# The query projection of a hybrid encoder layer as two units of seven block products, with the scores of two heads between the second unit's products

## The chip, the cores and the metric

The kernel runs on one core of one Trainium2 chip (trn2). The metric is the device time of one execution in microseconds; lower is better. The profile comes from one profiled execution on the same core. TensorE is PE (its weight loads are PEld), VectorE DVE, ScalarE ACT, GpSimd POOL, SyncE SP; SP issues most DMAs, POOL those that add to their destination.

## The reference, cut to what matters

One layer: a mixer (an S5 scan and a gated MLP, merged by gates) whose output goes through w_out and is added to the residual x; cross-attention to 256 memory tokens; a SwiGLU FFN; a last norm. 512 tokens of 1024 channels, 4 attention heads of 256, all float32. What the change touches:

```
def memory_cross_attention(hn, memn, w_q, w_k, w_v, w_o):
    bsz, seq, _ = hn.shape
    q = (hn @ w_q).reshape(bsz, seq, XATTN_HEADS, XATTN_HEAD_DIM)
    k = (memn @ w_k).reshape(bsz, MEM_LEN, XATTN_HEADS, XATTN_HEAD_DIM)
    v = (memn @ w_v).reshape(bsz, MEM_LEN, XATTN_HEADS, XATTN_HEAD_DIM)
    s = jnp.einsum('blhd,bmhd->bhlm', q, k).astype(jnp.float32) * (XATTN_HEAD_DIM ** -0.5)
    p = jax.nn.softmax(s, axis=-1).astype(v.dtype)
    o = jnp.einsum('bhlm,bmhd->blhd', p, v).reshape(bsz, seq, D_MODEL)
    return o @ w_o
...
        h = h + merged @ w_out[i]
        h = h + memory_cross_attention(rms_norm(h, xattn_norm_g[i]), memn,
                                       w_q[i], w_k[i], w_v[i], w_xo[i])
        h = h + swiglu(rms_norm(h, ffn_norm_g[i]), w_gate[i], w_up[i], w_down[i])
```

## The kernel before, in words

Every large product runs as three matmuls on pairs of rounded halves. `split` (line 85) makes such a pair of a float32 tile: ACT casts it to `hi` (line 87), DVE subtracts to get `lo` (line 88); `mm3` (line 319) then multiplies hi by hi, hi by lo and lo by hi.

**Weights.** All weight blocks stand in one list, `plan`, in the order of their use. Each entry has its loads and how many entries ahead they are issued (`LOADS`, 3, for plain loads into `wraw`; 4 to 7 for the tiles `b` and `t` of the units), and a function that splits the block into `whi` and `wlo`, two entries ahead of its use (`SPLITS`, line 93). `raw`, `hi` and `lo` have three buffers each. `next_w` (line 294) hands out the next block and triggers the loads and splits that are due. `feat` (line 324) multiplies with the weights at rest and gives channels by tokens, `tokm` (line 361) with the tokens at rest and gives tokens by channels. `tick` (line 414) lets code that was put off by `later` (line 404) run after a given amount of PE work. Within that, the order on each engine is made by the tile framework's scheduler when the kernel is built.

**Stages around the change.** w_out with the residual and the norm into `hn` (transposed on PE into `ptr`, split by `to_feat`); w_k (`feat`, 8 blocks of 4 x 128 rows by 256 columns, 128x256 matmuls, as there are 256 memory tokens); w_v (`tokm`); then for each of four heads two blocks of w_q, the head's scores with the softmax, and the values of the head before (`values`, tiles `po`, result split into `ot`), the turn of the probabilities (`turn_probs`, transposes into `ppt`, split into `p`) put off by one tick. Then w_xo (`tokm`), with the last head's values as its hook, and the norm for the FFN.

**Units.** Gate and up run as ten units of Strassen's scheme in Winograd's form: a 1024 by 512 block of the weights in four quarters, the tokens in four quarters, seven products of 24 matmuls of 128x256 (`product`, line 1273) in place of eight, with sums of quarters made on DVE (the weights') or once (the tokens'). Down does the same over chunks; its weight sums are made in DRAM ahead of time: for each of 24 jobs SP copies a block inside DRAM into `dsum` and POOL's DMA adds a second one onto it. `plan_sums` (line 224) hangs these jobs on entries of `plan`: the copies on every third entry from `first_copy + 2`, each addition three entries later.

**Memory.** Tiles of long life lie in slots: `hn` and later `fn` in B, `mg_hi` and `ot_hi` in D, `mg_lo`/`ot_lo` in E. `APART` (48, 112) are two offsets by which the units' pairs of halves begin apart. PSUM has five banks for products and three for transposes.

Of the kernel before, what the change touches and what calls it, by code (L numbers as in the profile page):

```python
# [52 lines left out]
def hybrid_layer_kernel(  # L53
# [140 lines left out]

    def plan_units(units, down):
# [28 lines left out]
    def plan_sums(first, step):  # L224


        more = {5: lambda c: down_block(0, 1, c), 7: lambda c: down_block(1, 1, c),
                6: lambda c: down_sum(5, c), 4: lambda c: down_sum(6, c)}

        def start(q, i, jc, c):  # L230
            tc.keep_in_program_order(nc.sync.dma_start(down_sum(q, c), down_block(i, jc, c)))

        def add(q, c):
            nc.gpsimd.dma_start(down_sum(q, c), more[q](c), accum_op=ALU.add)

        j = first
        for q, i, jc in ((5, 0, 0), (7, 0, 1), (6, 1, 1), (4, 1, 0)):
            for c in range(CHUNKS):
                plan[j][1].append((0, lambda x=(q, i, jc, c): start(*x)))
                plan[j + step][1].append((0, lambda x=(q, c): add(*x)))  # L240
                j += step
# [39 lines left out]
    for c0 in range(0, D, 256):  # L281
        plan_feat(w_q, c0, KD)
# [8 lines left out]
    plan_sums(first_copy + 2, 3)  # L291
# [176 lines left out]
    def to_feat(src, hi, lo, tsl, full=None):  # L468

        for q in range(2):  # L470
# [4 lines left out]
            split(hi[:, 4 * q:4 * q + 4, tsl], lo[:, 4 * q:4 * q + 4, tsl], ps)  # L475
# [5 lines left out]
    def norm_feat(src, g, hi, lo, tsl, ss=None, full=None):  # L481
        xs = xsp[0].tile([P, D], F32, tag="xs", name="xs", bufs=2)
        rms_scale(src, g, xs, ss)
        later(0.6, lambda: to_feat(xs, hi, lo, tsl, full))
# [580 lines left out]
    hn_hi, hn_lo = token_slot("hn")  # L1065
    hn = (hn_hi, hn_lo)
# [16 lines left out]
    for t in range(NM):  # L1083
        later(0.2 + t, lambda t=t: mem_norm(t))

# [15 lines left out]
    def feat_norm(g, hi, lo, full=None):  # L1101
        return lambda t, ss: norm_feat(h[:, t, :], g, hi, lo, slice(t * P, (t + 1) * P), ss, full)

    mg = (mg_hi, mg_lo)
    for half in range(2):
        tokm(w_out, half * 512, mg, KD, add_evac(half, 0, feat_norm(g_x, hn_hi, hn_lo)))
# [3 lines left out]
    shift = ap_.tile([P, APART[0]], F32, name="shift")  # L1110
    nc.gpsimd.memset(shift, 0.0)
    kt_hi = ap_.tile([P, KD, M], F32R, name="kt_hi")
    kt_lo = ap_.tile([P, KD, M], F32R, name="kt_lo")
    vt_hi = ap_.tile([P, NM, D], F32R, name="vt_hi")
    vt_lo = ap_.tile([P, NM, D], F32R, name="vt_lo")
# [4 lines left out]
    def v_evac(half):  # L1120
        def f(t, ps):
# [417 lines left out]
```

## Time and profile before

| | |
|---|---|
| time, median of 3 runs | 915.74 us (913.55 to 921.12) |
| the profiled execution's own time | 915.13 us |
| its span in the profile | 913.4 us |
| PE busy / idle in the span | 899.4 / 14.0 us |
| DVE, ACT, POOL busy | 608.1, 458.8, 90.8 us |
| w_k | 418.33 to 443.26 us |
| w_v | 443.26 to 465.66 us |
| w_q, scores, values 0 to 2 | 465.66 to 532.80 us |
| w_xo and the FFN's norm | 532.80 to about 583.5 us |

The span is cut at the first and last instruction; what lies around it makes 1.7 us. Stages are cut where the chain of work that ended last goes from one tile name to the next. Busy times are of one engine; PE and PEld overlap. In a row of the chain stand the start, the length, the engine, what was written, the line and how many instructions; in a row of groups, after the bar, the busy time of all and the mean ns of one.

### The profile page before, as it was taken

To read this page: it belongs to the slowest core of one execution; us is meant where nothing else is said; L and a number is where in the kernel's file an instruction comes from. 1 tells how busy PE (TensorE), PEld (TensorE's weight loads), DVE (VectorE), ACT (ScalarE), POOL (GpSimd) and SP (SyncE) were. 2 spreads that over 40 slices of the span, in tenths; PEclk is the share of its full clock that TensorE was granted. 3 is DMA by queue.
4 is the path that set the end of the run, shared out by engine and by line. 5 is a ranking of instruction groups with operands and counts; after the bars stand their busy time and mean duration, and the time that the engine had idled before them with its cause. 6 is when DMAs were issued, how large, how long until landed. Compare 5 with 4: busy or idle time off the path is not lost.

```text
span 913.4 us, 14223 instructions
## 1 busy us (share of the span) xinstructions
PE 899.4 (98%) x5558; PEld 789.9 (86%) x5558; DVE 608.1 (67%) x1003; ACT 458.8 (50%) x671; POOL 90.8 (10%) x153
## 2 busy tenths in 40 slices
PE   9999999999999999999999999999999999999996
PEld 6788888888888887789898888899999999888885
DVE  6596662888753235858545544787778777889875
ACT  5542995244374334446434433655554554655663
POOL 1004210000025300002010001000000000000000
PEclk9999999999999999999999999999999999999998
DMA  7445273684546655776995217416456453246572
GB/s 252 128 127 142 81 176 114 189 202 128 149 136 155 147 180 161 238 240 192 262 275 137 81 59 238 108 43 160 123 148 146 122 158 98 70 144 200 198 240 83
DMA packets 105557, 142.25 MB, mean 156 GB/s; under 512 B 13185, under 2 KB 73105, under 8 KB 105490
## 3 DMA queue, kind: packets, MB, share of 16 engines
q1 hardware_dynamic: 90690, 120.67, 40.7%
q0 software_dynamic: 12064, 19.37, 12.9%
q10 hardware_dynamic: 2736, 1.31, 0.6%
q8 instruction: 43, 0.70, 0.3%
q14 instruction: 24, 0.20, 0.1%
HBM read 134.54 MB, written 29.85 MB: 180 GB/s over the span
## 4 chain that ended last, share of the span: by engine, by line
PE 86%; ACT 4%; DVE 3%; DMA 3%; issue 2%; POOL 1%; POOLq 0%; SPq 0%; ACTq 0%; DVEq 0%
PE pf L322 32%; PE pt L322 13%; PE px L1282 12%; PE pq L1282 6%; PE dx L322 5%; PE dq L322 3%; PE pv L1282 3%; PE dv L322 2%; PE pk L731 2%; DVE wlo L88 1%; PE ptr L474 1%; DMA b<-in_w_gate_dram 1%; PE po L322 1%; ACT whi L87 1%; PE psc L322 1%
## 5 line engine op out<-in xcount | busy, mean ns | idle before, releaser
L88 DVE TENSOR_TENSOR wlo<-wraw,whi 128x1024 fp32r<-128x1024 f32 x132 | 157.4, 1193 | 132.4 <-ACT whi L87 131.2
L87 ACT CAST whi<-wraw 128x1024 fp32r<-128x1024 f32 x132 | 135.7, 1029 | 178.1 <-PE pf L322 81.7
L322 PE MATMUL pf<-xn,whi 128*128 128x512 f32 x448 | 140.7, 393 | 0.0
L322 PEld LDWEIGHTS pf<-xn,whi 128*128 128x128 f32 x448 | 83.7, 188 | 17.3 <-issue 0.2
L322 PE MATMUL pf<-xn,wlo 128*128 128x512 f32 x224 | 87.5, 391 | 0.0
L1282 PE MATMUL px<-fn,whi 128*128 128x256 f32 x480 | 83.7, 277 | 0.0
L1282 PEld LDWEIGHTS px<-fn,whi 128*128 128x128 f32 x480 | 72.7, 188 | 0.3 <-ACT u L1394 0.2
L87 ACT CAST whi<-b 128x1024 fp32r<-128x1024 f32 x40 | 42.2, 1054 | 54.5 <-PE px L1282 26.6
L88 DVE TENSOR_TENSOR wlo<-b,whi 128x1024 fp32r<-128x1024 f32 x40 | 48.9, 1222 | 27.3 <-ACT whi L87 27.3
L1282 PE MATMUL px<-fn,wlo 128*128 128x256 f32 x240 | 66.3, 276 | 0.0
L322 PE MATMUL dx<-whi,s 128*128 128x512 f32 x170 | 53.9, 392 | 1.4 <-ACT whi L87 1.0
L1282 PE MATMUL pq<-s,whi 128*128 128x256 f32 x320 | 55.0, 276 | 0.0
L322 PEld LDWEIGHTS pf<-xn,wlo 128*128 128x128 f32 x224 | 42.1, 188 | 8.5
L1282 PEld LDWEIGHTS pq<-s,whi 128*128 128x128 f32 x320 | 48.4, 188 | 0.1
L88 DVE TENSOR_TENSOR wlo<-t,whi 128x1024 fp32r<-128x1024 f32 x30 | 36.7, 1224 | 16.8 <-ACT whi L87 16.8
L87 ACT CAST whi<-t 128x1024 fp32r<-128x1024 f32 x30 | 31.6, 1054 | 32.2 <-PE pv L1282 11.3
L1282 PEld LDWEIGHTS px<-fn,wlo 128*128 128x128 f32 x240 | 45.1, 188 | 0.0
L1282 PE MATMUL pq<-s,wlo 128*128 128x256 f32 x160 | 44.2, 276 | 0.0
L322 PE MATMUL pt<-whi,xn 128*128 128x512 f32 x128 | 42.2, 402 | 0.0
L322 PE MATMUL pf<-hn,whi 128*128 128x512 f32 (+1 forms) x160 | 41.8, 348 | 0.0
L322 PEld LDWEIGHTS dx<-whi,s 128*128 128x128 f32 x170 | 31.7, 188 | 8.5 <-ACT whi L87 1.2
L322 PE MATMUL dx<-wlo,s 128*128 128x512 f32 x85 | 33.2, 391 | 0.2 <-DVE wlo L88 0.2
(384 smaller groups left out, 2170.1 us busy)
## 6 DMA issues: line engine op xcount, KB each, us to landing
wraw<-in_w_in_dram SPq DMA_DIRECT2D x36, 512.0 KB, 4.1
dsum<-in_w_down_dram SPq DMA_DIRECT2D x20, 512.0 KB, 5.9
wraw<-dsum SPq DMA_DIRECT2D x20, 512.0 KB, 3.9
b<-in_w_gate_dram SPq DMA_DIRECT2D x15, 512.0 KB, 3.6
b<-in_w_up_dram SPq DMA_DIRECT2D x15, 512.0 KB, 3.8
wraw<-in_w_down_dram SPq DMA_DIRECT2D x15, 512.0 KB, 3.6
dsum<-in_w_down_dram POOLq DMA_DIRECT2D x10, 512.0 KB, 6.4
dsum<-dsum POOLq DMA_DIRECT2D x10, 512.0 KB, 7.2
```

The lines of the kernel that those rows point to most:

```text
L87: nc.scalar.copy(dst_hi, src)
L88: last_lo[0] = nc.vector.tensor_tensor(dst_lo, src, dst_hi.bitcast(F32), ALU.subtract)
L322: nc.tensor.matmul(ps, a[x], b[y], start=start and i == 0, stop=stop and i == 2, skip_group_check=free)
L474: nc.tensor.transpose(ps[:, j, :], src[:, k * P:(k + 1) * P], ident)
L731: nc.tensor.matmul(ps[32 * j:32 * j + 32, q, :], bd[i][:, g].rearrange("p d c -> p (d c)"), lc(es[i], g), start=(i == 0), stop=False, tile ...
L1282: nc.tensor.matmul(ps[:, j, :], a[x], b[y], start=start and j == k == i == 0, stop=k == 3 and i == 2, skip_group_check=True)
```

## The change

w_q goes the units' way. Its 1024 columns are two units (n = 0, 1) of 512, heads 0 and 1 and heads 2 and 3; each is seven products. In the plan the 8 blocks of w_q become 14.

- **Weight sums** of the four products that need one (`qsum`, q = 4 to 7) are made in DRAM, 8 jobs more. They go first in the jobs' list; the places are new: 16 jobs on every third entry from `first_copy - 4`, two at 71 and 75, and the last 14 of down's at every fifth entry from 104, which lies in gate and up.
- **Token sums.** ACT copies each transposed `ptr` of hn into `hfull`, unrounded; `token_sums` makes four sums of quarters (128x1024 each) on DVE and splits them (`hsd`, `hse`, in slots D and E, and hn's own place), put off into w_k and w_v. Two of hn's own splits fall away. `hn` now lies `APART`.
- **Order.** Products 1, 5, 2, 6 and so on of both units are interleaved, with copies (`seed`, `kept`) and subtractions (`minus`) between, each finished part split at once into the head's query (`query_part`). scores(0) stands between products 6 and 7 of the second unit, scores(1) after the last. As `ot` lies in D and E, which hold token sums until the last product, values(0) and (1), scores(2) and (3) and the turns follow it; values(2) and (3) are w_xo's hook.
- **Places.** `hfull` and the memory values (`vt`) share one buffer; the probabilities of the odd heads take a buffer of the tag `gain`, so g_f is loaded later.

The core of the diff (`product` and `unit_bank` moved up with it, with the operands as an argument):

```
+    QSRC = {1: (0, 0), 2: (1, 0), 3: (1, 1)}
+    qsum = {(q, n): dp.tile([P, KD // 2, 256], F32, name=f"qsum{q}{n}") for q in (4, 5, 6, 7) for n in range(2)}
...
+        for q, n in ((1, 0), (5, 0), (2, 0), (6, 0), (1, 1), (7, 0), (2, 1), (4, 0), (3, 0),
+                     (6, 1), (7, 1), (5, 1), (4, 1), (3, 1)):
...
+                nc.sync.dma_start(got["raw"], query_block(*QSRC[q], n) if q in QSRC else qsum[q, n])
...
-    plan_sums(first_copy + 2, 3)
+    plan_sums([(first_copy - 4 + 3 * i, 3) for i in range(16)] + [(71 + 4 * i, 3) for i in range(2)] +
+              [(104 + 5 * i, 4) for i in range(14)])
...
-            split(hi[:, 4 * q:4 * q + 4, tsl], lo[:, 4 * q:4 * q + 4, tsl], ps)
+            if q != skip:
+                split(hi[:, 4 * q:4 * q + 4, tsl], lo[:, 4 * q:4 * q + 4, tsl], ps)
             if full is not None:
                 nc.scalar.copy(full[:, 4 * q:4 * q + 4, tsl], ps)
...
-    hn_hi, hn_lo = token_slot("hn")
+    hn_hi, hn_lo = token_slot("hn", APART)
...
+    def token_sums():
+        h11, h12, h21, h22 = (hfull[:, k, t] for t in (T0, T1) for k in (K0, K1))
+        for q, dst, x, y, op in ((5, h22, h21, h22, ALU.subtract), (7, h21, h11, h21, ALU.subtract),
+                                 (6, h11, h22, h11, ALU.subtract), (3, h12, h12, h11, ALU.add)):
+            nc.vector.tensor_tensor(dst, x, y, op)
+            later(0.5 * len(sums), lambda q=q, dst=dst: split(*hops[q], dst))
+            sums.append(q)
...
+    later(2, token_sums)
...
+        prob = ap_.tile([P, NT, M], F32, tag="prob", name="prob", bufs=1) if hd % 2 == 0 else \
+            np_.tile([P, NT, M], F32, tag="gain", name="prob", bufs=2)
...
-    for hd in range(XH):
-        feat(w_q, hd * XD, hn, KD, q_evac, parts=2 if hd == 0 else 1)
-        probs = scores(hd)
-        if hd > 0:
-            values(hd - 1, *pts.pop(0))
-        later(1, lambda hd=hd, probs=probs: pts.append(turn_probs(hd, probs)))
...
+    query_product(x1, 1, 6)
+    u2 = kept(x1, "u2")
+    probs0 = scores(0)
+    query_part(2, T0, v1)
+    query_product(x1, 1, 7)
+    u3 = kept(x1, "u3")
+    qq_ = unit_bank("qq")
+    query_product(qq_, 1, 5, True)
+    u3 = minus(qq_, u3)
+    query_product(x1, 1, 4)
+    query_part(2, T1, x1)
+    turn(0, probs0)
+    query_product(qq_, 1, 3)
+    u2 = minus(qq_, u2)
+    probs1 = scores(1)
+    query_part(3, T1, u3)
+    query_part(3, T0, u2)
+    ot_hi = slot("D", (P, KD, T), F32R, "ot_hi")
+    ot_lo = slot("E", (P, KD, T), F32R, "ot_lo")
+    values(0, *pts.pop(0))
+    probs2 = scores(2)
+    turn(1, probs1)
+    probs3 = scores(3)
+    values(1, *pts.pop(1))
+    turn(2, probs2)
+    later(1, lambda: turn(3, probs3))
...
-    tokm(w_xo, 0, ot, KD, add_evac(0, 1, None), hook=lambda: values(XH - 1, *pts.pop()))
+    tokm(w_xo, 0, ot, KD, add_evac(0, 1, None), hook=lambda: [values(i, *pts.pop(i)) for i in (2, 3)])
```

The scheduler makes of it three new neighbourhoods that the prediction speaks of. The first is DVE in w_k. Before, a block's `wlo` alternates with the remainders of w_k's result (`kt_lo`) and of hn:

```order
L88 TENSOR_TENSOR wlo<-wraw,whi 128x1024 [waits DMAHW3_49,PE_49,Activation_49]
L88 TENSOR_TENSOR hn<-ptr,hn 128x4x128 [waits Activation_49]
L88 TENSOR_TENSOR kt_lo<-pf_3864,kt_hi 128x256 [waits Activation_49]
L452 TENSOR_SCALAR ms<-ms 128x1 [waits DVE_49]
L88 TENSOR_TENSOR hn<-ptr,hn 128x4x128 [waits Activation_49]
L88 TENSOR_TENSOR wlo<-wraw,whi 128x1024 [waits DMAHW5_49,PE_49,Activation_49]
```

Now, at the middle of w_k:

```order
L88 TENSOR_TENSOR hn<-ptr,hn 128x4x128 [waits Activation_49]
L1166 TENSOR_TENSOR hfull<-hfull 128x4x256 [waits Activation_49]
L88 TENSOR_TENSOR wlo<-wraw,whi 128x1024 [waits DVE_49,DMAHW7_49,PE_49,Activation_49]
L1166 TENSOR_TENSOR hfull<-hfull 128x4x256 [waits DVE_49]
L88 TENSOR_TENSOR kt_lo<-pf_4030,kt_hi 128x256 [waits Activation_49]
L88 TENSOR_TENSOR hse<-hfull,hse 128x1024 [waits Activation_49]
L88 TENSOR_TENSOR wlo<-wraw,whi 128x1024 [waits DMAHW0_49,PE_49,Activation_49]
```

The sums (line 1166 of the changed kernel) and their remainders (`hse`, later `hsd`) stand one or two ahead of each `wlo`, from the fourth block of w_k into w_v.

The second is PE behind the last product. Before, a turn (`ppt`) stands amid w_q's products:

```order
L322 MATMUL pf_4781<-hn,whi 128x512
L1174 MATMUL ppt<-ident,prob 128x128 [waits DVE_49,PE_49]
L1174 MATMUL ppt<-ident,prob 128x128 [waits DVE_49]
L1174 MATMUL ppt<-ident,prob 128x128 [waits PE_49]
L1174 MATMUL ppt<-ident,prob 128x128
L1174 MATMUL ppt<-ident,prob 128x128 [waits DVE_49] x2
L1174 MATMUL ppt<-ident,prob 128x128 x2
L322 MATMUL pf_4781<-hn,whi 128x512
```

Now the tail of the scores of heads 2 and 3 (48 rows of `psc` in a row) is followed by the turns and, at once, by the values that need them:

```order
L341 MATMUL psc<-kt_lo,qq 128x256
L341 MATMUL psc<-kt_hi,qq 128x256
L1217 MATMUL ppt<-ident,prob 128x128 [waits DVE_49]
L1217 MATMUL ppt<-ident,prob 128x128
L1217 MATMUL ppt<-ident,prob 128x128 [waits DVE_49]
L1217 MATMUL ppt<-ident,prob 128x128
L1217 MATMUL ppt<-ident,prob 128x128 [waits DVE_49] x4
L341 MATMUL po<-p_hi,vt 128x512 [waits Activation_49]
L341 MATMUL po<-p_hi,vt 128x512
L341 MATMUL pt_5076<-whi,ot_hi 128x512
```

The turns wait for DVE's probabilities with only scores ahead of them, and `po` waits for ACT's cast of the turned ones; w_xo's first matmuls (`pt`) follow.

The third is SP at the FFN's entry, where the units' first loads are issued. Before, the last ones of them:

```order
L169 DMA b_5657<-in_w_up_dram 128x4x256
L169 DMA t<-in_w_up_dram 128x4x256
L169 DMA b_5725<-in_w_up_dram 128x4x256 [waits DMAHW7_49]
L169 DMA b_5142<-in_w_gate_dram 128x4x256 [waits DMAHW0_49,DVE_49]
L132 DMA wraw<-in_w_gate_dram 128x4x256 [waits DMAHW1_49,DVE_49]
```

Now:

```order
L169 DMA b_5811<-in_w_up_dram 128x4x256
L169 DMA t<-in_w_up_dram 128x4x256 [waits DMAHW6_49]
L258 DMA dsum_86<-in_w_down_dram 128x2x512 [waits DMAHW7_49]
L169 DMA b_5296<-in_w_gate_dram 128x4x256 [waits DMAHW0_49,DVE_49]
L169 DMA b_5880<-in_w_up_dram 128x4x256 [waits DMAHW1_49]
```

The load that PE needs first (b_5142 before, b_5296 now) has the same number of transfers ahead of it, but the last of them is now a copy inside DRAM, the first of down's late sums.

174 lines of the change are left out of this document (111 added, 63 removed).

## The prediction

> **What bounds the kernel now.** I read the page's busy table first, then the share of the clock by slices.
>
> ```profile
> span 913.4 us, 14223 instructions
> PE 899.4 (98%) x5558; PEld 789.9 (86%) x5558; DVE 608.1 (67%) x1003; ACT 458.8 (50%) x671; POOL 90.8 (10%) x153
> PEclk9999999999999999999999999999999999999998
> ```
>
> PE is busy 899.4 of 913.4 us at full clock: 14.0 us of idle in all. A change helps only by giving PE less to do, and hurts only by making PE wait. So next the busy time of each engine by stage; the columns are the span of the stage and then PE, PEld, DVE, ACT and POOL with the number of instructions, the granted clock, the DMA share and GB/s. The stages are w_k, w_v, w_q with scores and values, and w_xo with the entry to the FFN.
>
> ```profile
> 418.33:443.26 24.93, 24.93 (x217) 24.93 (x217) 20.66 (x31) 14.93 (x25) 3.34 (x4) 1.00 0.78 235
> 443.26:465.66 22.40, 22.40 (x99) 18.15 (x98) 11.91 (x12) 10.26 (x12) 1.61 (x2) 1.00 0.93 265
> 465.66:532.80 67.14, 66.98 (x397) 59.12 (x397) 34.43 (x62) 27.52 (x55) 3.24 (x4) 1.00 0.51 142
> 532.80:583.50 50.70, 50.26 (x232) 40.56 (x230) 24.77 (x40) 19.91 (x39) 3.77 (x4) 1.00 0.53 145
> ```
>
> The stage that the change rewrites, 465.66 to 532.80, holds PE for 66.98 of 67.14 us. Nothing there waits; only its matmuls can go. The w_k stage ahead of it has DVE at 20.66 of 24.93 us, so little room for more. The chain of work that ended last gives the rate of each matmul form.
>
> ```profile
> 465.66 11.50 PE pf L322 x96
> 432.90 10.37 PE pf L322 x88
> 612.69 2.72 PE pq L1282 x24
> 814.32 14.96 PE dq L322 x66
> 530.68 2.12 PE psc L322 x18
> 504.83 0.87 PE ppt L1174 x8
> 529.30 1.38 PE po L322 x6
> ```
>
> A 128x256 matmul takes 119.8 ns where head 0 of w_q reads hn (11.50/96), 117.8 ns in w_k (10.37/88), and 113.3 ns in the units of gate and up, whose halves of the tokens lie apart by the offsets 48 and 112 (2.72/24). A 128x512 one takes 226.7 ns (14.96/66).
>
> **Term 1, the products.** Before, w_q is 96 matmuls of 128x256 (head 0) and 144 of 128x512 (heads 1 to 3): 11.50 + 144 x 0.2267 = 44.14 us. After, it is 14 products of 24 matmuls of 128x256: 14 x 2.72 = 38.08 us. That is 6.06 us less. Two products fewer of 16 make 2 x 2.72 = 5.44 of it; the other 0.62 is head 0's slower rate, which hn's new offsets should cure. If they don't, that part is zero, so the term lies between -5.44 and -6.06; I take -6.06, since the unit that the new code copies shows 2.72 us. The four scores, turns and values stay what they are (2.12 us for 18, 0.87 for 8, 1.38 for 6): they are only moved.
>
> The Trainium skill, page "TensorE: Matmul & The Clock Gate", section "Wait — 56ns, not 53.3ns?", says that a warm matmul takes N / 2.4 GHz and a fixed 2.5 ns more, so that a column in a short matmul costs more. By it two of 256 would cost 2.5 ns more than one of 512, and the gain would be an estimated 4.9 us (336 x 109.2 ns against 96 x 109.2 and 144 x 215.8). The trace speaks against it: 226.7 is twice 113.3 within 0.1 ns.
>
> **Term 2, the token sums.** Four sums and their splits are added where w_k and w_v run. DVE and ACT rows (mean ns of one, behind the busy time of the group):
>
> ```profile
> L88 DVE TENSOR_TENSOR wlo<-wraw,whi 128x1024 fp32r<-128x1024 f32 x125 | 152.6, 1222 | 131.7 <-ACT whi L87 130.4 <-issue 0.8
> L806 DVE TENSOR_TENSOR wsx<-wsx,etmp 128x1024 f32<-128x1024 f32 x8 | 9.8, 1222 | 0.1
> L88 DVE TENSOR_TENSOR kt_lo<-pf,kt_hi 128x256 fp32r<-128x256 f32 x8 | 3.3, 415 | 0.0
> L88 DVE TENSOR_TENSOR hn<-ptr,hn 128x512 fp32r<-128x512 f32 x8 | 5.4, 680 | 0.0
> L87 ACT CAST whi<-wraw 128x1024 fp32r<-128x1024 f32 x125 | 131.3, 1052 | 173.3 <-PE pf L322 81.7 <-PE pt L322 28.1 <-issue 18.5
> L477 ACT COPY full<-ptr 128x512 f32<-128x512 f32 x8 | 4.7, 588 | 3.4 <-DVE fn L88 3.4
> ```
>
> DVE gets four sums and four subtractions of 128x1024 and loses two of 128x512: 8 x 1.22 - 2 x 0.68 = 8.4 us. ACT gets 8 copies and 4 casts and loses two casts: 8 x 0.59 + 4 x 1.05 - 2 x 0.59 = 7.7 us; it is at 14.93 of 24.93 and bears that. DVE's is the tight one: a w_k block holds PE for 24 x 0.1178 = 2.83 us and DVE for 1.22 + 0.42 = 1.64, so 1.2 us are free in each block, and w_k has eight, with hn's own remainders and the norms in the first four. Queued behind a sum on DVE stands the next wlo, and PE's next block waits for that. The weights are split two blocks ahead, some 5.7 us of cover; walked row by row, the backlog is eaten up just as w_v starts, whose blocks last twice as long and whose DVE is free for 10.5 us. I take 0.3 us. Below nothing it can't go; above, what doesn't fit: 8.4 less the room in the last four w_k blocks (4 x 1.2 = 4.8) is 3.6, less 1.2 at the first w_v block: 2.5.
>
> **Term 3, the tail.** Before, heads follow one another, and a head's softmax and turn run behind the next head's products. After, scores(2) and (3), values(0) and (1) and two turns stand together behind the last product, as ot's place is taken by the token sums until then. A softmax runs on DVE and ACT by these rows:
>
> ```profile
> L1158 DVE TENSOR_REDUCE mx<-psc 128x2 f32<-128x512 f32 x8 | 5.5, 692 | 5.3 <-PE psc L322 4.9
> L1161 ACT ACTIVATE prob<-psc,nm 128x256 f32<-128x256 f32 x16 | 7.4, 473 | 8.1 <-DVE nm L1159 8.1
> L1161 ACT ACTIVATION_READ_ACCUMULATOR prob<-psc,nm 128x1 f32 x16 | 3.2, 202 | 0.0
> L1165 DVE TENSOR_SCALAR prob<-prob,rs 128x256 f32<-128x256 f32 x16 | 4.9, 350 | 0.3
> L87 ACT CAST p_hi<-ppt 128x512 fp32r<-128x512 f32 x8 | 4.3, 589 | 1.4 <-PE ppt L1174 1.4
> L88 DVE TENSOR_TENSOR p_lo<-ppt,p_hi 128x512 fp32r<-128x512 f32 x8 | 5.1, 683 | 0.8 <-ACT p_hi L87 0.8
> ```
>
> From a pair's last score to its probabilities: 0.69 + 2 x (0.47 + 0.20) + 2 x 0.35 and two small steps, some 3 us; from the turn to the values 0.59 + 0.68. What stands between on PE is one head's 24 scores, 24 x 0.1178 = 2.83 us, where before it was half a head's products of 10.88. So a turn waits some 0.3 us; values(1) follow right behind the turns and wait for p_hi, 0.6; and where w_xo takes up values that were just evicted, 0.7 more. I take 1.6 us. At least 0.5 is lost, as p_hi can't be ready before its cast ends; at most each of the three waits is a whole eviction (0.59 + 0.68), 3 x 1.27 = 3.8, with 0.2 for scheduling: 4.
>
> **Term 4, DMA at the FFN's entry.** There the chain goes through one load, its cast and its remainder:
>
> ```profile
> 561.68 10.82 DMA b<-in_w_gate_dram
> 572.58 1.06 ACT whi L87
> 573.66 1.22 DVE wlo L88
> 560.00:565.00 5.00, 5.00 (x23) 4.13 (x22) 2.85 (x4) 2.33 (x7) 1.33 (x1) 1.00 1.05 351
> 570.00:575.00 5.00, 4.99 (x26) 3.89 (x25) 2.75 (x4) 1.05 (x1) 0.54 (x1) 1.00 1.18 250
> 545.00:550.00 5.00, 5.00 (x24) 4.08 (x23) 1.39 (x2) 1.33 (x2) 0.00 (x0) 1.00 0.47 164
> ```
>
> All DMA engines are full while it is on its way. The change puts a copy of down's weights inside DRAM right ahead of this load on SP, in place of a plain load of b. By the queue's mean (below) both take 1.6 us; if the copy, which also writes DRAM, takes as much again, 1.6 more. g_f's load moves to behind w_xo's sixth, where the engines still have room (0.47). I take 0.5 us, 0 to 2.4.
>
> **Term 5, DMA elsewhere.** Eight more copies and accumulates are made, and 14 of down's move into the units:
>
> ```profile
> q1 hardware_dynamic: 90690, 120.67, 40.7%
> q0 software_dynamic: 12064, 19.37, 12.9%
> dsum<-in_w_down_dram SPq DMA_DIRECT2D x20, 512.0 KB, 5.9
> dsum<-dsum POOLq DMA_DIRECT2D x10, 512.0 KB, 7.2
> 660.00:680.00 20.00, 20.00 (x179) 20.00 (x178) 14.80 (x14) 11.03 (x14) 1.27 (x1) 1.00 0.54 142
> 740.00:760.00 20.00, 20.00 (x179) 20.00 (x178) 14.72 (x16) 11.10 (x14) 1.27 (x1) 1.00 0.52 137
> ```
>
> 40.7% of 913.4 us for 120.67 MB is 3.1 us per MB, or 1.6 for 0.52 MB; POOL's accumulates cost 6.1 per MB, 3.2 each. Fourteen jobs in 165 us add 14 x 4.8 = 67 us, a share of 0.41 on top of 0.54: near full, but the loads are issued four blocks of 2.72 us ahead and land in 3.6, so about 7 us of cover hide it. On POOL, which runs in order, an accumulate waits for its copy of 5.9 us, asked for four blocks (10.9 us) earlier: done in time. I take 0, between 0 and 3 (one load late in each second of the last units by 0.6). Early on the eight new jobs take the places of old ones, with one more wait of SP for POOL: 0, from -1 to 1.
>
> **The sum.** -6.06 + 0.3 + 1.6 + 0.5 + 0 + 0 = -3.66 us. The profiled execution took 915.13 us around a span of 913.4; the median of the runs is 915.74, 0.61 above. So 911.5 on the profile's own time, and 912.1 as a median. With every term at its good end, -6.06 + 0 + 0.5 + 0 + 0 - 1 = -6.6: 909.2.
>
> **Rivals.** One hundredth, 9.2 us, is about what a measurement of this kernel can tell from no change, and the most that the change can save is 6.1.
> - All waits are covered: the tail finds other matmuls (PE idles only 0.16 us in this stage now) and SP's copy is no longer than the load. Then 915.74 - 6.06 + 0.5 = 910.2. Against it: the row order after the change has turns directly behind scores.
> - The tail is paced by the softmax. Its mechanism: with 24 scores between a pair and its turn, PE waits out the rest of a chain of 3 + 0.44 + 1.27 = 4.7 us for each of heads 1 to 3. It decides as soon as DVE's queue (p_lo, query remainders and softmax steps) is over 2.83 us behind. Then 3 x 4.7 = 14.1 less one head that the wlo's cover: some 9.4 lost for 6.06 won, 915.74 + 3.4 + 0.8 = 919.9, slower than before. For it: 8.1 us of ACT's idle stand before prob now; against: nothing on PE waited for them.
> - DMA is full in the units: at 0.95 the loads come late once an accumulate overlaps them, a product's weights arrive 1 us late in each of nine units, and 912.1 + 9 = 921. It decides when a load of b lands in over 10.9 us, as it does at the entry (10.82). For it: 0.54 + 0.41; against: the entry has eight transfers at once, the units two.
> - The fixed cost per matmul is real: 4.9 saved for 6.06, 913.3. Against it, the two rates above.
>
> **Numbers.** The forecast, 0.52; all covered, 0.18; tail, 0.14; DMA, 0.12; fixed cost, 0.04. The predicted time is 912.1. The range, 908.8 to 918.5, leaves out some 0.15 above it, over half of the tail's and DMA's cases (all terms at their bad ends, -5.44 + 2.5 + 4 + 2.4 + 3 + 1 = +7.5, would be 923.2), and some 0.03 below. Faster by over 1% (below 906.6) is out of reach of the products: 0.02. Slower by over 1% (above 924.9) needs the tail and DMA cases together or one at twice its price: 0.06. Within 1%: 0.92.
>
> **What would show it.** In the changed profile each product should read 2.72 us for 24 matmuls; at 2.83 or more, term 1 is short. PE's idle should rise from 14.0 by about 2.4 us, most of it before ppt and po (waiting for prob and p_hi). w_k and w_v should end within 0.5 us of their 47.3 us in all. The load at the FFN's entry should land within 13 us, and no px or pq in the units should wait for whi. If the time is over 915.7, the tail or the units' DMA share will show where: PE's idle before po, or whi's idle behind DMA.

## The result, and the profile after

The changed kernel takes 920.62 us, the median of 16 runs (914.53 to 926.09), beside 915.36 us for the kernel before (16 runs, 911.47 to 921.12): a ratio of 1.0059, with a 95% interval from 1.0038 to 1.0080. It is slower by 0.6%, which is within the 1% of "no change", but above the predicted range and of the other sign. The changed kernel's 16 times fall in two groups of eight, 914.5 to 919.8 and 921.4 to 926.1; of the 16 of before only one lies above 919. The median of the changed kernel lies in the gap between its groups, where none of its times is. The profiled execution, 918.45 us, is of the lower group.

The page after, in the rows shown of before:

```profile
span 916.6 us, 14519 instructions
PE 896.9 (98%) x5654; PEld 792.7 (86%) x5654; DVE 624.4 (68%) x1019; ACT 474.5 (52%) x693; POOL 101.0 (11%) x161
PEclk9999999999999999999999999899999999999999
```

PE is busy 2.5 us less, where 6.06 less were forecast, and idle 19.7 us for 14.0. One slice of the clock, the thirtieth, stands at 8: it lies at the entry to the FFN. Where PE's idle went is in the waits of PE; none of those shown here is in the kernel before (waited for, us in total, times, longest):

```profile
PE qx L1238 <- ACT u L1255: 2.7, 1, 2.7
PE pf L341 <- ACT fn L87: 2.2, 1, 2.2
...
PE pt L341 <- ACT ot_hi L87: 0.7, 1, 0.7
PE ppt L1217 <- DVE prob L1208: 0.6, 1, 0.6
...
PE pf L341 <- DVE fn L88: 0.4, 1, 0.4
```

The third and fourth are the tail that I had priced at 1.6: 1.3 us. The first, and the second with the last behind it at the same place (2.6 us together), I had not priced. The names behind the arrows (u, fn) are those of casts that came last; what held those casts up stands in the chain of waits. For the first:

```profile
454.46 6.48 DMA wraw<-in_w_q_dram
463.38 5.76 DMA wraw<-qsum
470.32 1.24 DVE wlo L88
471.58 8.73 DMA wraw<-in_w_q_dram
...
481.45 0.49 ACT u L1255
481.99 3.09 PE qx L1238 x24
486.14 2.83 PE qv L1238 x24
```

Three loads of w_q stand one behind the other in the chain; each was asked for when a `wlo` of DVE gave its raw buffer back, and they took 6.48, 5.76 and 8.73 us. The third came at 480.3; its cast stands on ACT ahead of `u`, the copy by which the next product's bank comes free, so PE stood still for 2.7 us. The seven products behind this stop then read 2.83 us (the first one 3.09), those ahead of it 2.71 to 2.78. The windows show the DMA engines full just then, and PE's loss (columns as before: span, PE, PEld, DVE, ACT, POOL, clock, DMA share, GB/s); the last three of them are the FFN's entry and the units:

```profile
464.00:468.00 4.00, 4.00 (x30) 3.70 (x29) 2.48 (x3) 1.23 (x3) 0.00 (x0) 1.00 1.06 300
...
480.00:484.00 4.00, 2.01 (x17) 2.01 (x18) 2.31 (x2) 2.96 (x4) 0.00 (x0) 1.00 0.40 115
...
582.00:585.00 3.00, 1.26 (x4) 0.97 (x5) 2.14 (x3) 2.08 (x4) 0.00 (x0) 0.73 0.00 0
585.00:588.00 3.00, 3.00 (x15) 3.00 (x16) 2.58 (x7) 2.93 (x7) 0.54 (x1) 0.50 0.54 175
...
604.00:800.00 196.00, 196.00 (x1706) 194.84 (x1705) 151.55 (x150) 103.57 (x125) 20.94 (x20) 1.00 0.71 181
```

The second stop, in the chain at the FFN's entry and on into the first unit:

```profile
563.17 18.54 DMA wraw<-in_w_up_dram
...
581.78 1.05 ACT whi L87
...
584.09 0.61 DVE fn L88
584.74 5.07 PE pf L341 x22
...
600.06 16.32 PE pf L341 x144
616.38 2.72 PE pq L1238 x24
```

Not the load of b of which I had written was late, but one behind it, a raw block of w_up: 18.54 us. `fn`'s cast is queued behind that block's cast on ACT, its remainder behind that block's `wlo` on DVE, and `fn` is the operand of the FFN's first product. PE then finds its clock at 0.73 and 0.50, so that 22 matmuls take 5.07 us where they took 2.87 before. In the units all is as forecast: 24 in 2.72 us, PE busy all the 196 us, at a DMA share of 0.71.

The profiled executions can be set against each other by stage, from the start of w_k (418.33 and 418.22) to the end:

| stage | before | after | difference | forecast |
|---|---|---|---|---|
| w_k, w_v, to the first product of w_q | 47.33 | 47.2 | -0.1 | +0.3 |
| w_q, tail and w_xo, to the end of the last values (554.69; 553.35) | 89.03 | 87.95 | -1.1 | -4.46 |
| to the FFN's first product (583.50; 584.74) | 28.81 | 31.39 | +2.6 | +0.5 (this row and the next) |
| to the first `pq` of the units (612.69; 616.38) | 29.19 | 31.64 | +2.4 | |
| units and all behind them, to the span's end | 300.7 | 300.2 | -0.5 | 0 |

That is +3.2 us of span for -3.66. The median rose by 5.3, so 2 us of it are not in this profile at all. The upper group of times is where to look for them, and the experiments were made for both.

### The profile page after: what moved, and what is told of

Same layout as the page of the kernel before. It is cut to its first block, busy times and chain, and to the rows that moved or that the text cites. A ratio compares the mean times of both kernels' runs of the same rounds, so it can differ in the third digit from the quotient of the medians.

```text
span 916.6 us, 14519 instructions
## 1 busy us (share of the span) xinstructions
PE 896.9 (98%) x5654; PEld 792.7 (86%) x5654; DVE 624.4 (68%) x1019; ACT 474.5 (52%) x693; POOL 101.0 (11%) x161
## 4 chain that ended last, share of the span: by engine, by line
PE 81%; DMA 6%; DVE 5%; ACT 5%; issue 2%; POOL 1%; POOLq 0%; SPq 0%; ACTq 0%; DVEq 0%
PE pf L341 26%; PE px L1238 12%; PE pt L341 11%; PE pq L1238 6%; PE dx L341 5%; PE dq L341 3%; PE pv L1238 3%; DVE wlo L88 2%; DMA wraw<-in_w_up_dram 2%; DMA wraw<-in_w_q_dram 2%; PE dv L341 2%; ACT whi L87 2%; PE qx L1238 2%; PE pk L751 2%; PE ptr L493 1%
## 5 line engine op out<-in xcount | busy, mean ns | idle before, releaser
L88 DVE TENSOR_TENSOR wlo<-wraw,whi 128x1024 fp32r<-128x1024 f32 x138 | 164.8, 1195 | 121.0 <-ACT whi L87 120.2
L87 ACT CAST whi<-wraw 128x1024 fp32r<-128x1024 f32 x138 | 142.0, 1029 | 171.9 <-PE pf L341 64.5
L1238 PEld LDWEIGHTS pq<-s,wlo 128*128 128x128 f32 x160 | 30.1, 188 | 0.0
```

Source lines behind the costliest of these rows:

```text
L87: nc.scalar.copy(dst_hi, src)
L88: last_lo[0] = nc.vector.tensor_tensor(dst_lo, src, dst_hi.bitcast(F32), ALU.subtract)
L1238: nc.tensor.matmul(ps[:, j, :], a[x], b[y], start=start and j == k == i == 0, stop=k == 3 and i == 2, skip_group_check=True)
```

## The experiments: the two stops

The theory was that jobs in DRAM (a copy on SP, an accumulate on POOL) fill the DMA engines at two places where a load has no cover. The jobs that stand there are down's, which the eight new ones of w_q have pushed to later places. Rivals: DVE is late from the token sums and gives the raw buffers back late; and the late transfers themselves slow the units. "Ticks" below are the program's own count of blocks, by which jobs are placed; the late jobs stood at 104, 109, and so on.

**e1: late sums begin behind the entry.**

```
-               [(104 + 5 * i, 4) for i in range(14)])
+               [(114 + 4 * i, 4) for i in range(14)])
```

> The changed kernel (920.6 us); the 14 late jobs of down's weight sums begin at entry 114 of the plan and come every 4 entries (before: 104, every 5), so that no copy and no accumulate of them is issued among the FFN's first loads; the two jobs in w_v and w_q stay. Theory: at the FFN's entry PE lost 5.0 us against the kernel before, 2.56 by standing idle until a load that one copy and one accumulate had delayed (18.5 us to landing), and 2.45 by the lower granted clock that followed (0.84 from 584 to 604 us). Then the idle there falls under 0.6 us, the clock stays at 1.00, and the time is about 915.6 (914 to 917.5). Rival: the entry's loads are late from g_f's new place and their own number, and the clock fell by chance: idle stays over 1.5 us and the time over 918.5.

Measured: 919.36 us, ratio 1.0029 (1.0003 to 1.0054); four runs from 911.4 to 913.7, eight from 917.5 to 921.7. The median misses the 914 to 917.5 that were expected, as two thirds of the runs lie in the upper group. In its profile (912.14 us) the stop at the entry is gone, and the drop of the clock with it; the stop of `qx` is still there, 2.8 us. The window of the entry:

```profile
584.00:604.00 20.00, 20.00 (x178) 20.00 (x177) 17.00 (x21) 12.69 (x20) 0.55 (x1) 1.00 0.18 54
```

PE is busy all 20 us at clock 1.00, and the raw block of w_up lands 14.5 us after its issue, where it took 18.5 with the jobs and 14.4 in the kernel before. So the jobs at the entry made that stop; g_f's new place, the rival, is the same here. With the stop gone the lower group moves from 917.3 (the median of the eight) to 912.6 (of the four).

**e2: no sums beside w_q.** The two jobs at ticks 71 and 75 go to the late ones, which still begin at the entry.

```
-    ... + [(71 + 4 * i, 3) for i in range(2)] + [(104 + 5 * i, 4) for i in range(14)])
+    ... + [(104 + 4 * i, 4) for i in range(16)])
```

> The changed kernel; the two jobs that were at entries 71 and 75 (copies at 452.6 and 463.8 us, accumulates at 459.9 and 470.8 us) go to the late ones, which are now 16, from entry 104 every 4; the FFN's entry keeps its copy and accumulate. Theory of the copies: these two jobs filled the DMA engines (share 0.82 to 1.06 from 452 to 480 us) and made w_q's fourth load take 8.73 us; without them PE's idle of 2.72 us before qx falls under 0.7 and the time falls by some 2.3, to about 918.3. Rival, the backlog on DVE: the token sums held back the remainders that free the raw buffers, so the loads of w_v and w_q were issued late (DMA share only 0.40 to 0.53 from 440 to 452 us); then the idle stays at 1.5 us or more and the time at about 920.

Measured: 916.80 us, 1.0013 (0.9984 to 1.0043); five at 910.1 to 912.4, seven at 916.4 to 921.1. The wait of `qx` is gone, and w_q's products all run in 2.72 to 2.74; the stop at the entry stays (1.3 and 0.8 us). Its profile, 919.55 us, fell in the upper group, and shows what that group is. From the chain:

```profile
594.14 16.96 PE pf L340 x144
611.11 2.83 PE pq L1237 x24
```

24 matmuls take 2.83 us: 117.8 ns each instead of 113.3, though PE waits for nothing. From the first `pq` of the units to the last this makes 201.6 us of 194.7.

**e3: both moved.** Sixteen late jobs, from tick 114.

```
-    ... + [(71 + 4 * i, 3) for i in range(2)] + [(104 + 5 * i, 4) for i in range(14)])
+    ... + [(114 + 4 * i, 4) for i in range(16)])
```

> Both of the above in one: 16 late jobs from entry 114, every 4 entries; none in w_v, w_q or at the FFN's entry. If both theories hold the gains add up: 920.6 - 5.0 - 2.3 = 913.3, some 2 us faster than before (915.4). If only the entry matters: 915.6. If sixteen jobs in fewer entries fill the DMA engines in the units, PE idles there before px or pq and the time stays over 917.

Measured: 915.18 us, 0.9979 (0.9950 to 1.0009); four at 908.3 to 908.6, seven at 914.9 to 918.0. In the profile (908.52) no product waits. From the chain:

```profile
465.48 2.74 PE qx L1237 x24
...
590.09 16.32 PE pf L340 x144
606.41 2.72 PE pq L1237 x24
```

From the first product of w_q to the end of the last values it takes 83.83 us, 5.2 less than before. This is the gain that terms 1 and 3 had forecast (4.46) and 0.7 more, and 6.6 us of the profiled time are won against before. The median does not show it, because seven of eleven runs are in the upper group.

**e7: token sums a block later**, 0.6 ticks apart, and pinned in their place on DVE, to tell DVE's backlog from the jobs in DRAM.

```
-    later(2, token_sums)
+    later(3.0, token_sums)
```

> The changed kernel with the four token sums and their remainders traced one block later, 0.6 ticks apart and pinned in that order on DVE, so that the first five blocks of w_k have none ahead of their remainders and the last ones reach into w_v. Same work, same DMAs. Theory of the backlog on DVE: the raw buffers of w_k's middle blocks are freed sooner, the DMA share from 440 to 452 us rises over 0.5, and the idle before qx falls by a us or more: about 919. Theory of the copies: the idle stays at 2.7 and the time at 920.6.

Measured: 917.67 us, 1.0026 (1.0000 to 1.0052). The wait of `qx` falls from 2.7 to 0.7 us, and 0.6 are new at `qv`; the DMA share from 440 to 452 us is 0.44, not raised as I had expected. So the stop in w_q needs both: DVE, busy 4.00 of 4.00 us when w_v starts, gives the raw buffers back late, and the loads then fall on the two jobs. Without the jobs (e2) the backlog costs nothing; with the sums later the jobs cost half. That the raw buffers came back sooner in e7 is not shown, as the DMA share did not rise. Nor are the jobs alone enough: the kernel before has four copies and five accumulates issued from 440 to 482 us, at a DMA share of 0.91 up to 480, and PE waits for none of its loads there. A third condition is new, and no run tests it by itself: a block of w_q held PE for 5.4 to 5.75 us before and holds it for 2.72 now, so each load has half the cover.

**e4: the kernel before with 14 late sums.**

```
-    plan_sums(first_copy + 2, 3)
+    plan_sums([(first_copy + 2 + 3 * i, 3) for i in range(10)] + [(104 + 5 * i, 4) for i in range(14)])
```

> The kernel before (914.5 us) with only the places changed: ten of down's 24 jobs stay early, the last 14 go to entries 104, 109 and so on, as in the changed kernel; here none of them falls among the FFN's first loads. What is open: single times of the changed kernels fall into two groups some 7 us apart, and in one profile of the upper group every product of the units took 2.83 us for 24 matmuls (117.8 ns each), in all others 2.72 (113.3 ns); 1700 such matmuls make 7.6 us. Before, about 1 time in 9 is in the upper group, in the changed kernels 7 to 8 of 12. If the late transfers bring the slow rate, half or more of the times lie near 922. If what stands ahead of the units brings it, at most 2 of 12 do, and the median is 914.5.

Measured: 914.93 us, 1.0017 (0.9999 to 1.0034); ten at up to 915.8, two at 921.0 and 922.3. The units run at 113.3 ns at a DMA share of 0.80 from 620 to 800 us (before 0.49), and PE is as busy there as before (178.98 of 180 us in both):

```profile
620.00:800.00 180.00, 178.98 (x1551) 177.43 (x1550) 138.72 (x137) 96.75 (x116) 22.07 (x21) 1.00 0.80 196
```

So late transfers do the units no harm. For the stop at the entry this run says nothing: w_q has 8 blocks here and not 14, so tick 104 comes later in the layer, and the first late copy is issued at 618.58 us, behind the entry (in the changed kernel at 557.85).

**e5: the kernel before, hn with the offsets 48 and 112.**

```
-    hn_hi, hn_lo = token_slot("hn")
+    hn_hi, hn_lo = token_slot("hn", APART)
```

> The kernel before with one line changed: hn's halves lie apart by the units' offsets (48, 112). The prediction put 0.62 us of its first term here: head 0's 96 matmuls of 128x256 from 119.8 to 113.3 ns each (11.50 to 10.88 us). Theory: that, so 913.9 in median and 10.88 us for the 96 in the profile. Rival: the rate of these matmuls isn't set by the offsets; they stay at 117.8 or more, and the time at 914.5.

Measured: 914.57 us, 0.9998 (0.9987 to 1.0010). Head 0's 96 matmuls take 10.90 us for 11.50: the 0.6 of term 1 is there, and too small to show in the median.

## The experiments: the two rates in the units

Theories at the start: the transfers slow PE's matmuls; a memory or a clock that drifts; or a phase that TensorE is left in by the rows ahead, and that it keeps until some row changes it.

**e9: the changed kernel without down's sums.** Their copies and accumulates are left out, and the four products of down that need a sum load a plain block of the same size, so the output is not the reference's.

```
-                    src = down_block(*DSRC[q], c) if q in DSRC else down_sum(q, c)
+                    src = down_block(*DSRC.get(q, (q // 4 % 2, q % 2)), c)
```

> The changed kernel with down's 24 weight sums left out altogether (copies and accumulates; down's four products that need a sum load a plain block of the same size in its place, so the output is not the reference's). w_q's eight sums stay. It takes all late transfers away, the entry's and w_q's with them. Theory of the late transfers: the lower group takes nearly all times, and the median is that group's 908.4. Theory of what stands ahead: half or more stay in the upper group, median about 915. Both: no idle over 0.7 us before qx or at the FFN's entry.

Measured: 912.47 us, 0.9953 (0.9926 to 0.9980), in two groups again: five at 904.3 to 907.0, seven at 912.4 to 914.9. The profile is of the upper group:

```profile
588.45 16.96 PE pf L336 x144
605.41 2.83 PE pq L1233 x24
```

No transfer of a sum is left in the units, and their rate is 117.8. These transfers are not the cause; the loads of plain blocks are still there.

**m1: the rate alone.** Only products of the units' form, with rows of other kinds between them (four transposes, 6 to 9 matmuls of 128x512, pauses of 1 to 4 copies on ACT); all else of the layer is left out.

> The rate of the products by itself: a kernel that only loads three blocks of w_gate and x, splits them, and runs the units' products (24 matmuls of 128x256 in groups of three on halves) six at a time, pinned in order, with one of these between the sixes: nothing, four 128x128 transposes, six to nine 128x512 matmuls, or a pause (a matmul that waits for one to four copies on ACT); first with the tokens' halves apart by 48 and 112, at last with both at 0. All else of the layer is left out. If an interruption picks the rate, sixes of the same operands run at 113.3 ns a matmul after some and at 117.8 after others; a pause should bring the slow rate most often (in the changed kernel's w_q it came with a pause of 2.72 us). If only the offsets decide, all sixes with the halves apart take 113.3, those at 0 take 119.8. If it is the traffic of the other engines and DMA, all run at 113.3, as there is none here.

The chain, with the matmuls between the breaks:

```profile
46.95 16.35 PE pq L121 x144
...
64.69 16.34 PE pq L121 x144
...
131.63 1.62 PE wide L136 x7
133.25 16.97 PE pq L121 x144
...
332.39 17.29 PE pq L121 x144
```

The two rates of the layer appear with next to no transfers (a DMA share of 0.02 at most in any 4 us of theirs): 113.5 ns after four transposes, after 6 and after 8 wide ones; 117.8 after 7 and after 9. Pauses of one to three copies kept the rate, and the one of four led from 117.8 to 113.3; that a pause brings the slow rate, as expected, did not come true. With both halves of the tokens at offset 0 there is one rate, some 120 (17.29/144). 117.8 is also the mean of one matmul at 113.3 and two at 120.0, and each group has three; but the trace speaks against such a mixture, as the starts in the slow stretch are an even 117 to 119 ns apart, whichever half is read. "Odd counts bring the 117.8 ns, four transposes the 113.3" was the theory for the next kernels.

**e12: e3 and four transposes ahead of the units' loop; e14: the changed kernel with the same; e15: the kernel before with four transposes and seven wide matmuls.**

```
+    mark = aux("mark", (P, 4, P))
+    for j in range(4):
+        tc.keep_in_program_order(nc.tensor.transpose(mark[:, j, :], ones, ident))
     for i, u in enumerate(UNITS):
```

> Both places moved (groups at 908.4 and 915.7, 7 of 11 in the upper one), and four 128x128 transposes of ones pinned right ahead of the units' loop (0.4 us of PE). In the kernel that only ran products, each six after four transposes took 113.5 ns a matmul, also where the six before it had taken 117.8. Theory: the transposes set the fast rate, so all executions fall into the lower group: 908.9 in median (908 to 910), 5.5 us under the kernel before, and the units' products read 2.72 us. Rival: they flip the rate, or do nothing in this place; then the groups stay, with a median of 909 or 916 by their shares.

> The changed kernel as it is, and the same four transposes ahead of the units' loop. Its stalls in w_q and at the FFN's entry stay. Theory: of its 5.3 us over the kernel before, some 3.5 come from the units' rate, which is slow in half of its executions, and these go: median 917.3 (914.5 to 919.5), and no times over 921. Rival: 920.6 as before.

> The kernel before with the four transposes and then seven 128x512 matmuls (an odd number) pinned ahead of the units' loop; their results are used by nothing. They cost 0.4 and 1.6 us of PE. In the kernel that only ran products, the six after seven or nine such matmuls ran at 117.8 ns, after six or eight at 113.5. Theory: the odd number brings the slow rate into every execution: 914.4 + 2.0 + 7.2 = 923.6, units' products at 2.83 us. Rival: it was the pause or chance; then 916.4.

Measured: e12 916.21 us, 1.0003 (0.9975 to 1.0030), eleven of twelve runs in the upper group; e14 916.85, 1.0043 (1.0005 to 1.0080), eight at 914.5 to 918.4 and four at 921.2 to 927.1; e15 916.32, 1.0017 (0.9992 to 1.0041), all at 914.3 to 918.0. From the chain of e12:

```profile
590.12 16.96 PE pf L340 x144
607.08 0.44 PE mark L1478 x4
607.52 2.83 PE pq L1237 x24
```

And of e15:

```profile
596.19 16.33 PE pf L322 x144
...
614.57 2.74 PE pq L1282 x24
```

Four transposes leave the rate where it was, and four with seven wide ones behind them do too. The theory fell. What these rows do show is that the rate is there before the units' loop, in the 144 `pf` ahead of it. The starts in e12's trace place its beginning more closely: the ten `pv` from 586.73 us are 113 to 114 ns apart, four `ptr` transposes follow, and the `pv` from 588.22 are 117 to 119 apart. The profiles of e2 and e9 read the same at this place; in e3 both stretches of `pv` come to 113.

**e11: e3 with one matmul more, of ones, pinned ahead of the FFN's first product.**

> Both places moved, as in the kernel that measured 915.2 us in median with groups at 908.4 and 915.7, and one 128x128 matmul of ones into a PSUM bank of its own pinned ahead of the FFN's first product: it adds under 0.3 us of PE, shifts the order of PSUM banks by one, and holds the scheduler from mixing px with the first gate matmuls. If the rate of the units hangs on this neighbourhood the share of the upper group changes: the median goes to 908.5 to 909, under the kernel before by 6 us; if not, it stays at 915.

Measured: 917.85 us, 1.0040 (1.0016 to 1.0064), six at 913.5 to 915.1 and six at 920.6 to 922.3. The pin made PE wait 3.6 us for a transpose's operand, so it changed more than the count, and says little.

**m2: which break turns the rate.** Again products alone; each of eleven kinds of break five times, in five orders: one to four transposes, one to four wide matmuls, four transposes inside a product after 10 or 13 matmuls, and a pause of one copy.

> The kernel that only runs products, again, all else of the layer left out: threes of products (72 matmuls of 128x256, halves apart by 48 and 112), and between them, in an order that changes, five times each: one to four 128x128 transposes, one to four 128x512 matmuls, four transposes inside a product after 10 or 13 matmuls, a pause of one copy on ACT. Each stretch gives the rate before and after one interruption. Theory: the rate is a phase that an interruption shifts by its own length; then each kind either keeps or changes the rate in the same way each time, 1 and 3 wide matmuls change 113.5 to 117.8, 2 and 4 keep it, and four transposes give 113.5. Rival: chance; the same kind leads now to the one, now to the other rate from the same start.

From the chain (72 matmuls in 8.17 us are the rate of 113, in 8.48 that of 118):

```profile
130.16 8.48 PE pq L127 x72
138.64 0.23 PE wide L142
138.87 8.17 PE pq L127 x72
...
500.65 8.17 PE pq L127 x72
508.82 0.11 PE ptr L137
508.93 8.49 PE pq L127 x72
```

One transpose turned the rate into the other one in all five places, three did too, and one wide matmul; two transposes led from 113 to 118 five times; four transposes and four wide ones led to 113 from either; a pause of one copy kept it. Of the theory, that one and three wide matmuls change the rate holds in nine places of ten; four wide ones do not keep it. The same kind from the same rate gave the same but for two places of 55: two wide matmuls and three wide ones, from 118, led twice to 113 and once stayed. So the rate acts as a phase that PE's rows move on, and is not chance. The single transpose is the handle to try in the layer.

**e17: e3 and one transpose; e18: e3 and four wide matmuls; e19: the kernel before and one transpose; e20: the changed kernel and one transpose**, each ahead of the units' loop.

```
+    mark = aux("mark", (P, 4, P))
+    tc.keep_in_program_order(nc.tensor.transpose(mark[:, 0, :], ones, ident))
     for i, u in enumerate(UNITS):
```

> Both places moved, and one 128x128 transpose of ones (0.1 us) pinned right ahead of the units' loop. In the kernel that only ran products one transpose changed the rate from whichever it was to the other, five times of five. Without a mark, and with four transposes, 18 of 23 executions lay in the upper group here. Theory of the phase: the shares change places, about 9 of 12 lie in the lower group, at 908.6, and the median is there, 5.5 us under the kernel before; in the profile the gate's rest and the units' products take different rates. Rival: what a single transpose did there doesn't carry over to these operands; the median stays at 915.5.

> The same place, four 128x512 matmuls on fn (0.9 us) instead of the one transpose. In the kernel that only ran products the stretch after four of these ran at 113.5 ns five times of five, from either rate. Theory: all executions in the lower group, now at 909.3, median 909.5. Rival: as with the four transposes, which did the same there and nothing here: median 916.5.

> The kernel before, and the one transpose (0.1 us) pinned ahead of the units' loop, nothing else. It ran its units at the fast rate in about 9 of 10 executions. Theory of the phase: the transpose changes the rate, so about 9 of 10 now run at 117.8 ns: median 922 (914.5 + 0.1 + 7.3), products of 2.83 us in the profile. Rival: before, something else holds the fast rate (its memory or its order); then 914.6.

> The changed kernel as it was delivered, and the same one transpose. Its stalls stay, so the groups stay at about 917 and 924, half of the executions in each; after pauses of changing length the phase ahead of the loop is left to chance. Theory: the shares change places, which here changes little: median 917 to 922. If it falls to 917 and no time lies over 920, the slow rate was the more frequent one in it.

| kernel | median us | ratio to before (95%) | times |
|---|---|---|---|
| e3 | 915.18 | 0.9979 (0.9950 to 1.0009) | 4 at 908.3-908.6, 7 at 914.9-918.0 |
| e17 | 909.92 | 0.9962 (0.9937 to 0.9987) | 9 at 907.2-910.8, 3 at 914.5-916.0 |
| e18 | 916.37 | 1.0016 (0.9994 to 1.0037) | all at 914.5-917.3 |
| e19 | 921.39 | 1.0072 (1.0047 to 1.0098) | 1 at 914.0, 6 at 920.6-922.1 |
| e20 | 918.77 | 1.0052 (1.0022 to 1.0083) | 7 at 913.1-918.9, 5 at 920.5-925.2 |

The chain of e17:

```profile
590.94 16.96 PE pf L340 x144
607.90 0.11 PE mark L1477
608.01 2.75 PE pq L1237 x24
```

And of e19, whose profile is its one time of 914.0:

```profile
594.99 16.96 PE pf L322 x144
611.95 0.11 PE mark L1375
612.06 2.75 PE pq L1282 x24
```

In both the products ahead of the transpose run at 117.8 and those behind it at 113.3 ns: one row of 0.11 us turned the phase. For the other direction, 113 to 118, m2 has the profile and the layer has the times. On e3, whose units mostly run at 117.8, it brings nine of twelve times into the lower group; on the kernel before, which mostly runs at 113.3, it puts six of seven into the upper one: 7 us for a row of 0.11. With e12 and e18, where other rows in the same place leave 11 and 12 of 12 times in the upper group, that settles that the phase, and not the transfers or the added work, makes the upper group. e17 is faster than both kernels, each taken by its ratio to before, if only by 0.4% of before: 0.9962 (0.9937 to 0.9987) of before, while the changed kernel is 1.0059 (1.0038 to 1.0080). In e20 both groups remain in nearly equal number. That fits a phase that differs from run to run behind the stop at the entry, so that one turn only exchanges the groups; it is not shown by itself. Four wide matmuls, which in m2 led to 113 from either, left e18 at 2.83 us for 24, with all its times in the upper group.

## Why the prediction was wrong, step by step

- **Term 1, the products (-6.06), held where nothing stops them.** 14 products at 2.72 us stand in e3, and e5 shows hn's 0.6 by itself. In the changed kernel the seven products behind the stop run at 2.83 us, up to the turns at 504.87 us, and so do the scores between them at 117.8 ns a matmul; this costs about 1 us more.
- **Term 2, the token sums (+0.3), held for its own stage (-0.1) and missed its consequence.** I had asked what a late `wlo` does to PE's next block. It also gives a raw buffer back late, and with that moves three loads of w_q onto the two jobs in DRAM: 2.7 us. No term had w_q's loads in it. (Its upper bound holds a slip: 3.6 less 1.2 is 2.4 and not 2.5.)
- **Term 3, the tail (+1.6), held:** 0.6 and 0.7 of waits in the changed kernel and in e3. Products and tail together make -5.2 in e3, so the tail costs some 0.9 if the products give all of their 6.06. PE's idle rose by 5.7 us and not by the 2.4 forecast, and only 1.3 of it is ahead of `ppt` and w_xo. The rival that the softmax paces the tail came to 919.9, near the measured 920.62, by luck: none of its waits of 4.7 us is there.
- **Term 4, the DMA at the FFN's entry (+0.5, at most 2.4), is the step that failed,** with 5.0 us. It followed the one load that ended last in the chain of before, b. That load landed after 11.1 us (before 10.8), within the 13 that were to be the sign of this term; its place as the last was taken by the raw block behind it, at 18.54 us. I priced the copy as one transfer ahead of one load, by the queue's mean, while all engines were full and two transfers more made another load land after 18.5 us where it takes 14.5 without them (e1). The second is the accumulate that POOL issues at 566.58 us, which the term left out; and neither its 0.5 nor its 2.4 was worked out from a row, only the 1.6 between them. The price of the wait was left as its length: behind 2.6 us of it the clock is down, and the slower clock costs 2.4 more. e1 and e3 take the jobs away from there, and both parts go.
- **Term 5, DMA elsewhere (0), held in the units:** 194.7 us both times, no late load at a share of 0.71, and the rival of full DMA there is out by e4 as well. It was wrong, with 2.7 us and the slow products behind them, for the two early jobs beside w_q, for which "take the places of old ones" stood in place of a look at what loads then.
- **What no term had: the phase.** Half of the changed kernel's runs lie in the upper group, some 7 us longer. No profile of it fell there; those of e2, e9, e12 and e18 in their upper groups all read 117.8 ns in the units. I had taken the 113.3 ns of the units' profile as a property of the operands' offsets. It is one of two rates that the same rows have, and with the change to the rows ahead of the units the odds are others: eight of 16 runs for one of 16.
- **The rival of a fixed cost per matmul** has nothing for it: the products read 113.3 ns in e3 as in the units of before.

The sum of the known pieces in the profile: -3.66 forecast, +2.7 and +1 in w_q, +4.5 at the entry, make +4.5; the lighter tail, w_k and w_v and the end take 1.3 back: +3.2. The rest of the median's +5.3 fits the odds of the phase, half of the runs being in the upper group; no run shows it by itself.

Open: why the same four `ptr` at the entry leave 117.8 ns in one execution and 113.3 in another; what in TensorE the phase is; why four transposes and four wide matmuls, which gave 113 among bare products, leave the layer's rate as it is.

## What to carry to other kernels

Where the DMA engines are full, price a new transfer by every load then under way, the ones behind the critical load too, and by what its cast holds up on its engine (here 2.2 us behind ACT); then ask whether the wait is long enough to cost the clock. Put added jobs where the trace shows room and nothing first-needed (here: behind the FFN's entry, which is worth 5 us). And before a change of under 1% is believed, compare how one matmul form reads in several runs: if it has two rates, the odds of each are part of the result, and a row of 0.11 us can be worth 7 us, with either sign.

## What the runs showed of the hardware

**Two rates, and a phase.** 128x256 matmuls of the same operands run at 113.3 or 117.8 ns, for hundreds of microseconds on end, with nothing waited for, at a granted clock of 1.00. A single transpose changes the one into the other: from 117.8 to 113.3 in the profiles of e17 and e19, and both ways in m2, five times of five.

**The clock falls after shorter waits than I had thought, and not always.** In m1, where PE paused for a chain of copies, two pauses apart in length:

```profile
152.00:156.00 4.00, 4.00 (x36) 4.00 (x35) 0.00 (x0) 0.00 (x0) 0.00 (x0) 1.00 0.02 4
...
224.00:228.00 4.00, 4.00 (x24) 4.00 (x23) 0.00 (x0) 0.00 (x0) 0.00 (x0) 0.57 0.00 0
```

After 1.38 us (two copies) the clock stays at 1.00; after 2.03 us (three) it is 0.57 in the next 4 us. In the layer, the stop at the entry, 2.6 us by its two waits, brought 0.50, and in e2 its 1.3 and 0.8 us brought 0.72 in the 4 us from 578 us; the stop of `qx`, 2.7 us, brought nothing. The Trainium skill, page "TensorE: Matmul & The Clock Gate", section "HAM oscillation — how this bites in real kernels", gives the rule as no gap of PE's idle above some 3.4 us. The 2.7 us of `qx` agree with it, and 2.0 us in m1 and 2.6 at the entry do not, as they were enough; so a gap of 2 us and more is to be counted as a risk.
